# One-hot gate matrix, top-k selection and rank inversion in 16 bits, with the gate in three 16-bit parts

## The chip, the cores and the metric

The kernel runs on one core of a Trainium2 chip. The metric is device time in microseconds (us); less is better. The core has five engines with a queue each: PE (TensorE, matmuls into the PSUM banks; its weight loads are a row of their own, PEld), DVE (VectorE, elementwise and reductions), ACT (ScalarE, activations, copies and scalings), POOL (GpSimd, here almost only a queue that issues DMAs) and SP (a queue that issues DMAs). An engine works through its queue in order; semaphores make it wait for other engines and for DMAs.

## The reference, cut to what matters

One encoder block over 256 tokens of width 2048: modulation, mixer (convolution and attention), and then a PEER layer, in which every token takes 16 of 16384 experts for each of 8 heads:

```python
scores = einsum('bshpd,hpnd->bshpn', q, sub_keys)          # two halves, 128 keys each
top_v, top_i = top_k(scores, 16)
cand = top_v[..., 0, :, None] + top_v[..., 1, None, :]      # 16 x 16 per head
best_v, best_i = top_k(cand, 16)
i1 = take_along_axis(top_i[..., 0, :], best_i // 16)
i2 = take_along_axis(top_i[..., 1, :], best_i % 16)
expert, gate = i1 * 128 + i2, softmax(best_v)
a   = einsum('td,tnd->tn', h, peer_u[expert])
out = einsum('tn,tnd->td', gelu(a) * gate, peer_v[expert])
```

## The kernel before, in words

The kernel does not gather rows of `peer_u`. In its **block loop** it multiplies all 256 tokens with all 128 blocks of 128 experts: for a block, 1 MB of `peer_u` comes in on SP's queue (`ru`, 4 buffers `wraw`), ACT rounds it to `hu` (L198), DVE makes the remainder `lu` (L199), and PE runs 48 matmuls of 128x256 (`mm3`: L213 and L214 with `hu`, then L217 with `lu`) into `pu`. ACT writes GELU of it to `A` (L1185). `hu` and `lu` have two buffers each.

Beside this stream runs the **gate part** (`side_steps`), a generator that the block loop advances by a budget: every block pays SIDE = 3.3, and each `yield` says what its step costs, so this table of costs sets how many steps stand between two blocks. A Tile scheduler then orders each engine's queue. Its steps, for each half of 128 tokens (`tt`): top-k of the 256 sums (`cand`), selection of the indices with a one-hot `eq` (L927 compares, L931 multiplies, L933 sums), softmax, a transpose through PE (`selT`, L944), and then the **gate matrix**: for each token a 128x128 matrix with the gate at (i2, i1), as a product of two one-hot matrices. In steps of four tokens DVE compares a counter `iota` with `i2T` and with `i1T` (`oh_make`, L869, two instructions of 512 elements), ACT scales the second one by the gate, token by token (L872), PE multiplies (`oh_use`, L882, one f32 matmul per token), ACT copies the result to `stage` (L884), and after each 16 tokens DVE takes the largest value over them (L890 or L893), which tells the sort which experts are in use. HOLD = 2 says how many steps lie between the making and the use of a one-hot pair. The gate part has the first UPART = 48 blocks; what is left of it then is issued at once.

In the later blocks a second generator, `sort_steps`, orders the experts by which token groups use them. It ends with the **inversion** of the ranks: 32 steps of four one-hot rows, two comparisons (L1090), two products (L1092, L1093) and four matmuls of 128x256 in 16 bits (L1082). At the same time `ask` and `weigh` bring the gate matrix back, multiply it into `A` and put the result to HBM (`actd`); both issue on POOL's queue. At block EARLY_AT = 118 seven gathers of 1 MB of `peer_v` (`fetch_raw`, `rv` and `early`) go onto POOL's queue, and behind them the load `bt` of the last gate's bias, for which four additions on DVE (L977) wait.

After the block loop comes the **product stage** (`po`, L1228 and L1236): for each sorted block 1 MB of `peer_v` and its weights (`mc`) are gathered through POOL's queue and multiplied. Then the sum, the last norm and the output.

Of the kernel before, what the change touches and what calls it, by code (L numbers as in the profile page):

```python
# [21 lines left out]
T = 256  # L22
# [7 lines left out]
UPART = 48  # L30
ABUFS = 7
E2BUFS = 4
HOLD = 2
# [21 lines left out]
EARLY_AT = NBLK - 10  # L55
# [75 lines left out]
def hybrid_block_kernel(  # L131
# [34 lines left out]
    def ps_tile(name):  # L166
# [5 lines left out]
    iota = cst.tile([128, 128], F32, name="iota")  # L172
    nc.gpsimd.iota(iota, pattern=[[1, 128]], base=0, channel_multiplier=0,
                   allow_small_or_imprecise_dtypes=True)
# [68 lines left out]
    with tc.tile_pool(name="pre", bufs=1) as pre:  # L243
# [5 lines left out]

        vec = pre.tile([128, NVEC], F32, name="vec")  # L250
# [566 lines left out]
    sifs = [tks[:, 1024 + i * 256:1280 + i * 256].rearrange("p (h k) -> p h k", k=16) for i in range(2)]  # L817

    def m1(name, dt=F32):
        return sp.tile([128, 256], dt, tag="m1", name=name, bufs=5)  # L820
# [36 lines left out]
    i1T, i2T, gT = [m1(n) for n in ("i1T", "i2T", "gT")]  # L857
# [4 lines left out]
    def oh_make(tt, q):  # L862
        t = tt * 128 + q * 4
        it = iota.unsqueeze(1).to_broadcast([128, 4, 128])
        ohs = []
        for i, src in enumerate((i2T, i1T)):
            oh = e2(f"oh{tt}_{q}") if i else work[:, 2048 + 512 * ((32 * tt + q) % 3):][:, :512]
            oh = oh.rearrange("p (t i) -> p t i", t=4)
            V.tensor_tensor(oh, it, src[:, t:t + 4].unsqueeze(2).to_broadcast([128, 4, 128]), ALU.is_equal)  # L869
            ohs.append(oh)  # L870
        for j in range(4):
            S.activation(ohs[1][:, j], ohs[1][:, j], AF.Copy, scale=gT[:, t + j:t + j + 1])  # L872
        return ohs

    def oh_use(tt, q, ohs):
        tb, qq = divmod(q, TB // 4)
        if qq == 0:
            stages[tt, tb] = g8(f"stage{tt}_{tb}", (128, 128, TB))
        stage = stages[tt, tb]
        p = ps_tile(f"gps{tt}_{q}")  # L880
        for j in range(4):
            keep(PE.matmul(p[:, j * 128:(j + 1) * 128], lhsT=ohs[0][:, j], rhs=ohs[1][:, j],  # L882
                          start=True, stop=True))
        S.activation(stage[:, :, qq * 4:(qq + 1) * 4].rearrange("p i t -> p t i"),  # L884
                     p.rearrange("p (t i) -> p t i", t=4), AF.Copy)
        if qq == TB // 4 - 1:
            S.dma_start(gd[tt * (128 // TB) + tb], stage)
            gm = picked[:, 4 * tt + tb * TB // 32]
            if tb * TB % 32 == 0:
                V.tensor_reduce(gm, stage, AX.X, ALU.max)  # L890
            else:
                mx = e2(f"mx{tt}_{tb}")[:, :128]
                V.tensor_reduce(mx, stage, AX.X, ALU.max)  # L893
                V.tensor_tensor(gm, gm, mx, ALU.max)

    def side_steps():
# [5 lines left out]
        for tt in range(2):  # L902
# [16 lines left out]
            for which in range(2):  # L919
                if which == 0:  # L920
                    V.tensor_single_scalar(bs, bi, 4, ALU.logical_shift_right)
                else:
                    V.tensor_single_scalar(bs, bi, 15, ALU.bitwise_and)
                bf = tk[:, 1536:1664].rearrange("p (h k) -> p h k", k=16)
                V.tensor_copy(bf, bs)
                eq = g8(f"eq{tt}_{which}", (128, 8, 16, 16))
                V.tensor_tensor(eq, bf.unsqueeze(3).to_broadcast([128, 8, 16, 16]),  # L927
                                iota[:, :16].unsqueeze(1).unsqueeze(1).to_broadcast([128, 8, 16, 16]),
                                ALU.is_equal)
# [16 lines left out]
            V.tensor_copy(i1T[:, ts_], pt[:, 0:128])  # L946
            V.tensor_copy(i2T[:, ts_], pt[:, 128:256])
            V.tensor_copy(gT[:, ts_], pt[:, 256:384])
            yield 1.0
            for q in range(32):  # L950
# [4 lines left out]
                yield 1.2  # L955
# [26 lines left out]
    def sort_steps():  # L982
        nk = len(CLASSES) + 1
        cls = work[:, 2048:2048 + 64 * nk].bitcast(BF).rearrange("p (k i) -> p k i", k=nk)
        flat = sp.tile([128, 512], BF, tag="m1", name="tri", bufs=5)
# [86 lines left out]
        plo = work[:, 1024:1280].rearrange("p (c i) -> p c i", c=2)  # L1072
        V.tensor_copy(plo[:, 0], ri)
        V.tensor_copy(plo[:, 1], rj)
        yield 5.0
        pi = ps_tile("inv")
        it = iota.unsqueeze(1).to_broadcast([128, 4, 128])
        late = None

        def invert(ch, oh, vals):  # L1080
            for i in range(4):
                keep(PE.matmul(pi[:, :256], lhsT=oh[:, 0, i], rhs=vals[:, i].rearrange("p a b -> p (a b)"),  # L1082
                              start=(ch == 0 and i == 0), stop=(ch == 31 and i == 3)))

        for ch in range(32):
            isl = slice(ch * 4, (ch + 1) * 4)
            oh = sp.tile([128, 2, 4, 128], BF, tag="e2", name=f"sl{ch}", bufs=E2BUFS)
            vals = sp.tile([128, 4, 2, 128], BF, tag="e2", name=f"sv{ch}", bufs=E2BUFS)
            for i in range(2):
                V.tensor_tensor(oh[:, i], it, plo[:, i, isl].unsqueeze(2).to_broadcast([128, 4, 128]),  # L1090
                                ALU.is_equal)
            V.tensor_scalar(vals[:, :, 0], oh[:, 1], pidx, None, ALU.mult)  # L1092
            V.tensor_tensor(vals[:, :, 1], oh[:, 1], iota[:, isl].unsqueeze(2).to_broadcast([128, 4, 128]),  # L1093
                            ALU.mult)
# [3 lines left out]
            yield 2.4  # L1098
# [80 lines left out]
    for i1 in range(NBLK):  # L1179
# [260 lines left out]
```

## Time and profile before

| | |
|---|---|
| median of 3 runs | 1761.83 us (1760.68 to 1767.35) |
| profiled execution, whole | 1762.56 us |
| its span, first to last instruction | 1760.8 us |
| PE busy | 1683.4 us (96%) |
| DVE busy | 1200.5 us (68%) |
| ACT busy | 761.6 us (43%) |
| block loop | 565.5 to 1387.6 us |
| gate matrix of the first and the second 128 tokens | 641.1 to 743.6 and 800.5 to 910.5 us |

A matmul's recorded duration holds its way through the array, so the rate of PE is read from the starts of matmuls that follow one another, and what a stage costs from its length. In a timeline row the first number is the start and the second the length of a run of equal instructions, with the idle time before it and what ended it in brackets. In a row of groups come the count, then the busy time in us and the mean ns of one, then the engine's idle time before.

### The profile page before, as it was taken

The page shows a single profiled execution, that of the slowest core. Times are in us where ns is not written, and L with a number is a line of the kernel's source. Part 1 is how long each engine was busy: PE and PEld are TensorE (multiplying, and loading weights), DVE is VectorE, ACT ScalarE, POOL GpSimd, SP SyncE. Part 2 cuts the span into 40 slices and gives each one's busy share as a digit, 9 for nine tenths or more (in the row PEclk, how much of TensorE's full clock was granted, in tenths as well). Part 3 has the DMA queues.
Part 4 walks back from the last instruction along what each step waited for, and adds up shares of the span by engine and source line. Part 5 has one row for each costly group of instructions (what it writes and reads, how often), then busy time and mean ns, then how long its engine had stood idle before and what let it go on. Part 6 is the DMA issues. An engine that isn't in the chain of part 4 may idle for free. (4 is left out here: it accounts for less than half of the span.)

```text
span 1760.8 us, 29506 instructions
## 1 busy us (share of the span) xinstructions
PE 1683.4 (96%) x12507; PEld 1461.9 (83%) x12507; DVE 1200.5 (68%) x1605; ACT 761.6 (43%) x1016; POOL 288.1 (16%) x257
## 2 busy tenths in 40 slices
PE   4998999899999999999999999999999999999996
PEld 2778999899899999899999999999999754444542
DVE  6769899778667988897885788898744332222324
ACT  3233467334544468847974343333433232222322
POOL 0000000000000000000000000000030476756771
PEclk8988999899999999999999999999999999999998
DMA  9998888679555455546569887888988599998895
GB/s 396 425 375 298 324 331 304 244 277 348 207 217 180 158 182 212 195 175 219 198 233 347 284 307 255 296 298 286 322 311 317 219 393 393 354 361 336 307 395 217
DMA packets 77928, 505.93 MB, mean 287 GB/s; under 512 B 9472, under 2 KB 10112, under 8 KB 22496
## 3 DMA queue, kind: packets, MB, share of 16 engines
q1 hardware_dynamic: 44784, 319.82, 48.2%
q0 software_dynamic: 29712, 162.94, 25.3%
q10 hardware_dynamic: 3296, 21.24, 3.0%
q8 instruction: 100, 1.64, 0.4%
q14 instruction: 36, 0.29, 0.0%
HBM read 466.21 MB, written 37.75 MB: 286 GB/s over the span
## 5 line engine op out<-in xcount | busy, mean ns | idle before, releaser
L213 PE MATMUL pu<-h2hi,hu 128*128 128x256 f32 x2048 | 497.8, 284 | 0.0
L198 ACT ACTIVATE hu<-ru 128x2048 fp32r<-128x2048 f32 x128 | 245.4, 1917 | 365.7 <-PE pu L214 316.7
L213 PEld LDWEIGHTS pu<-h2hi,hu 128*128 128x128 f32 x2048 | 386.0, 188 | 0.6 <-issue 0.2
L199 DVE TENSOR_TENSOR lu<-ru,hu 128x2048 fp32r<-128x2048 f32 x128 | 293.1, 2291 | 135.6 <-ACT hu L198 133.4
L217 PE MATMUL pu<-h2hi,lu 128*128 128x256 f32 x2048 | 263.2, 281 | 0.5 <-DVE lu L199 0.5
L217 PEld LDWEIGHTS pu<-h2hi,lu 128*128 128x128 f32 x2048 | 251.3, 188 | 0.7 <-DVE lu L199 0.7
L214 PE MATMUL pu<-h2loT3a,hu 128*128 128x256 f32 x1024 | 249.4, 282 | 0.0
L214 PE MATMUL pu<-h2loT3b,hu 128*128 128x256 f32 x1024 | 247.9, 281 | 0.0
L1228 PE MATMUL po<-rv,mc 128*64 128x512 f32 (+2 forms) x1064 | 225.5, 600 | 5.2 <-PEq L1310 2.6
L1228 PEld LDWEIGHTS po<-rv,mc 128*64 128x64 f32 (+2 forms) x1064 | 72.6, 131 | 147.0 <-issue 140.5
L214 PEld LDWEIGHTS pu<-h2loT3a,hu 128*128 128x128 f32 x1024 | 193.2, 189 | 0.2 <-issue 0.2
L214 PEld LDWEIGHTS pu<-h2loT3b,hu 128*128 128x128 f32 x1024 | 192.9, 188 | 0.0
L1125 POOL DMA_DIRECT2D gg<-gd x16 | 18.7, 1169 | 914.9 <-DVE work L1002 914.6
L1170 POOL DMA_INDIRECT rv<-in_peer_v_dram,perm_idx x107 | 129.1, 1207 | 77.1 <-PE po L1228 33.2
L204 DVE TENSOR_TENSOR lv<-rv,hv 128x2048 fp32r<-128x2048 f32 x24 | 55.1, 2294 | 122.5 <-ACT hv L203 89.9
L1177 POOL DMA_INDIRECT mc<-actd,perm_idx x109 | 121.1, 1111 | 37.1 <-issue 30.8
L241 DVE SCALAR_TENSOR_TENSOR acc<-ada,cact,acc 128x2048 f32<-128x2048 f32 x45 | 105.7, 2348 | 3.4 <-DMA ada<-in_w_ada_dram 3.4
L203 ACT ACTIVATE hv<-rv 128x2048 fp32r<-128x2048 f32 x24 | 45.9, 1913 | 130.6 <-DMA rv<-in_peer_v_dram,perm_idx 118.4
L198 ACT ACTIVATE hwin<-rwin 128x2048 fp32r<-128x2048 f32 x33 | 63.0, 1910 | 66.1 <-DMA rwin<-in_w_in_dram 40.0
L213 PE MATMUL pwin<-hhi,hwin 128*128 128x256 f32 x336 | 88.4, 301 | 0.0
L872 ACT ACTIVATE oh<-oh,gT 128x128 f32<-128x128 f32 x256 | 80.8, 390 | 14.8 <-DVE oh L869 14.1
L204 DVE TENSOR_TENSOR third<-rv,third 128x2048 fp32r<-128x2048 f32 x12 | 27.6, 2299 | 87.3 <-ACT third L203 53.7
(522 smaller groups left out, 3036.3 us busy)
## 6 DMA issues: line engine op xcount, KB each, us to landing
ru<-in_peer_u_dram SPq DMA_DIRECT2D x128, 1024.0 KB, 5.4
ada<-in_w_ada_dram SPq DMA_DIRECT2D x96, 1024.0 KB, 7.4
rwin<-in_w_in_dram SPq DMA_DIRECT2D x33, 1024.0 KB, 6.1
rwout<-in_w_out_dram SPq DMA_DIRECT2D x16, 1024.0 KB, 5.3
rwq<-in_w_q_dram SPq DMA_DIRECT2D x16, 1024.0 KB, 4.8
gd<-stage ACTq DMA_DIRECT2D x16, 1024.0 KB, 5.0
gg<-gd POOLq DMA_DIRECT2D x16, 1024.0 KB
actd<-A POOLq DMA_DIRECT2D x15, 1024.0 KB
```

Of the source, the lines that this page charges most:

```text
L198: S.activation(hi, raw, AF.Copy)
L199: V.tensor_tensor(lo, raw, hi.bitcast(F32), ALU.subtract)
L203: S.activation(hi, src, AF.Copy)
L204: V.tensor_tensor(lo, src, hi.bitcast(F32), ALU.subtract)
L213: PE.matmul(dst, lhsT=whi[:, sl], rhs=rhi[:, c], start=(c == sets[0][0]), stop=False)
L214: PE.matmul(dst, lhsT=whi[:, sl], rhs=rlo[:, c], start=False, stop=False)
L217: PE.matmul(dst, lhsT=wlo[:, sl], rhs=rhi[:, c], start=False, stop=(c == sets[-1][-1]))
L241: V.scalar_tensor_tensor(acc, raw, cact[:, k:k + 1], acc, ALU.mult, ALU.add)
L872: S.activation(ohs[1][:, j], ohs[1][:, j], AF.Copy, scale=gT[:, t + j:t + j + 1])
L1170: keep(nc.gpsimd.indirect_dma_start(raw, None, v_rows, index(main[n])))
L1177: keep(nc.gpsimd.indirect_dma_start(ms[-1][:, n % 8], None, actd[:, :], index(main[n])))
L1228: keep(PE.matmul(po[tt * 4 + d4][row:row + size], lhsT=m[:, at * size:(at + 1) * size], rhs=raw[:, d4 * 512:(d4 + 1) * 512], start=start, ...
```

## The change

The counter `iota`, the indices and the one-hot matrices become 16-bit, and every index is written twice side by side (`twice`), so that the comparison with a row reads pairs of neighbouring 16-bit values on all three sides (`hot`). The steps of the gate matrix hold eight tokens in place of four (OHB). ACT's scaling goes; instead the gate is split into three 16-bit parts that add up to it (`gT` with three columns per token), one DVE instruction makes the three scaled one-hot matrices of eight tokens (3072 elements), and PE adds three 16-bit matmuls per token where one f32 matmul stood. The one-hot matrix for i2 moves from `work` to the `e2` buffers, the three products take two buffers in `work`, HOLD is 1, and the step's cost in the table is 2.6. The selection's `eq` and its index factor are 16-bit. The inversion has 16 steps of eight rows; its matmuls are 256 of 128x128 in place of 128 of 128x256. UPART is 50, and the seven early gathers are spread over the blocks 114 to 126, one at each even one; the rest of the sort is issued at 114.

```diff
-UPART = 48
+UPART = 50
-HOLD = 2
+HOLD = 1
+OHB = 8
-EARLY_AT = NBLK - 10
+EARLY_AT = (114, 116, 118, 120, 122, 124, 126)
...
+    i1T, i2T = [sp.tile([128, T, 2], BF, tag="m1", name=n, bufs=2) for n in ("i1T", "i2T")]
+    gT = sp.tile([128, T, 3, 2], BF, tag="gT", name="gT")
+
+    def hot(dst, idx):
+        n = idx.shape[1]
+        V.tensor_tensor(dst.rearrange("p n (a b) -> p n a b", b=2),
+                        pairs_of(iota).unsqueeze(1).to_broadcast([128, n, 64, 2]),
+                        idx.unsqueeze(2).to_broadcast([128, n, 64, 2]), ALU.is_equal)
+
+    def twice(x):
+        return x.unsqueeze(2).to_broadcast([128, x.shape[1], 2])
...
     def oh_make(tt, q):
-        t = tt * 128 + q * 4
-        it = iota.unsqueeze(1).to_broadcast([128, 4, 128])
-        for i, src in enumerate((i2T, i1T)):
-            oh = e2(f"oh{tt}_{q}") if i else work[:, 2048 + 512 * ((32 * tt + q) % 3):][:, :512]
-            V.tensor_tensor(oh, it, src[:, t:t + 4].unsqueeze(2).to_broadcast([128, 4, 128]), ALU.is_equal)
-        for j in range(4):
-            S.activation(ohs[1][:, j], ohs[1][:, j], AF.Copy, scale=gT[:, t + j:t + j + 1])
+        t = tt * 128 + q * OHB
+        oh2, oh1 = [e2(f"oh{i}_{tt}_{q}").bitcast(BF).rearrange("p (t i) -> p t i", t=OHB) for i in (2, 1)]
+        og = work[:, 1024 + 1536 * (q % 2):2560 + 1536 * (q % 2)].bitcast(BF).rearrange("p (t c i) -> p t c i", t=OHB, c=3)
+        hot(oh2, i2T[:, t:t + OHB])
+        hot(oh1, i1T[:, t:t + OHB])
+        V.tensor_tensor(og.rearrange("p t c (a b) -> p t c a b", b=2),
+                        oh1.rearrange("p t (a b) -> p t a b", b=2).unsqueeze(2).to_broadcast([128, OHB, 3, 64, 2]),
+                        gT[:, t:t + OHB].unsqueeze(3).to_broadcast([128, OHB, 3, 64, 2]), ALU.mult)
+        return oh2, og
...
         for j in range(4):
-            keep(PE.matmul(p[:, j * 128:(j + 1) * 128], lhsT=ohs[0][:, j], rhs=ohs[1][:, j],
-                          start=True, stop=True))
+            for c in range(3):
+                keep(PE.matmul(p[:, j * 128:(j + 1) * 128], lhsT=ohs[0][:, t0 + j], rhs=ohs[1][:, t0 + j, c],
+                              start=(c == 0), stop=(c == 2)))
...
+            left = tk[:, 1792:1920]
+            V.tensor_copy(gT[:, ts_, 0], twice(pt[:, 256:384]))
+            V.tensor_tensor(left, pt[:, 256:384], gT[:, ts_, 0, 0], ALU.subtract)
+            V.tensor_copy(gT[:, ts_, 1], twice(left))
+            V.tensor_tensor(left, left, gT[:, ts_, 1, 0], ALU.subtract)
+            V.tensor_copy(gT[:, ts_, 2], twice(left))
-            for q in range(32):
+            for q in range(128 // OHB):
...
-                yield 1.2
+                yield 2.6
...
-        for ch in range(32):
+        for ch in range(16):
...
-        if i1 == EARLY_AT:
+        if i1 == EARLY_AT[0]:
             for _ in side:
                 pass
-            for n in range(EARLY):
-                fetch_raw(n)
+        if i1 in EARLY_AT:
+            fetch_raw(EARLY_AT.index(i1))
```

**DVE, gate matrix of the first 128 tokens, before** (`lu` is the remainder of a block's weights, `work<-iota,i2T` and `oh_n` the two one-hot matrices of a step of four tokens):

```order
L199 TENSOR_TENSOR lu_6843<-ru_6840,hu_6842 128x2048
L869 TENSOR_TENSOR work<-iota,i2T 128x512
L869 TENSOR_TENSOR oh_8_6727<-iota,i1T 128x512
L869 TENSOR_TENSOR work<-iota,i2T 128x512
L869 TENSOR_TENSOR oh_9_6797<-iota,i1T 128x512
L199 TENSOR_TENSOR lu_6927<-ru_6924,hu_6926 128x2048
L893 TENSOR_REDUCE mx_1_6810<-stage_1_6706 128x128
L869 TENSOR_TENSOR work<-iota,i2T 128x512
```

The same place now (`oh_0_k` twice is the pair of step k, i2 first; `work<-oh,gT` is the product with the three gate parts):

```order
L198 TENSOR_TENSOR lu_6966<-ru_6963,hu_6965 128x2048
L910 TENSOR_REDUCE mx_1_6835<-stage_1_6715 128x128
L866 TENSOR_TENSOR oh_0_5_6894<-iota,i2T 128x1024
L911 TENSOR_TENSOR work<-work,mx_1_6835 128x128
L866 TENSOR_TENSOR oh_0_5_6895<-iota,i1T 128x1024
L866 TENSOR_TENSOR oh_0_6_6928<-iota,i2T 128x1024
L882 TENSOR_TENSOR work<-oh_0_5_6895,gT 128x3072
L198 TENSOR_TENSOR lu_7056<-ru_7053,hu_7055 128x2048
```

The comparison for step 6 now stands ahead of step 5's product, and the product is DVE's where ACT had it.

**PE, the end of step 4 and the beginning of step 5 there, now** (`gps` is a PSUM bank of four tokens, with three matmuls and three weight loads per token):

```order
L899 LDWEIGHTS oh_0_4_6801
L899 MATMUL gps_9_6914<-work,oh_0_4_6801 128x128
L899 LDWEIGHTS oh_0_5_6894
L899 MATMUL gps_10_6933<-work,oh_0_5_6894 128x128
L899 LDWEIGHTS oh_0_5_6894
L899 MATMUL gps_10_6933<-work,oh_0_5_6894 128x128
```

Two steps stand next to each other on PE, with no block between them; this is so at six places (steps 0 and 1, 4 and 5, 9 and 10 of the first half; 1 and 2, 5 and 6, 10 and 11 of the second), and everywhere else one block of 48 matmuls stands between two steps. Before, PE's queue had up to three banks of four tokens in a row, and single matmuls of a bank between single ones of a block.

**POOL, around the early gathers, now** (`actd` puts weighed `A` tiles, `gg` asks for gate matrix, `bt` is the bias):

```order
L1195 DMA rv_14023<-in_peer_v_dram,perm_idx 128x2048
L1195 DMA rv_14137<-in_peer_v_dram,perm_idx 128x2048
L1150 DMA gg_14251<-gd 128x16x128
L1195 DMA rv_14253<-in_peer_v_dram,perm_idx 128x2048
L994 DMA bt<-in_b_gtf_dram 128x2048
L1195 DMA rv_14382<-in_peer_v_dram,perm_idx 128x2048
L1161 DMA actd<-A_13851 128x8x256
L1150 DMA gg_14498<-gd 128x16x128
L1195 DMA rv_14500<-in_peer_v_dram,perm_idx 128x2048
```

Before, all seven gathers stood in one run ahead of `bt`; now three stand ahead of it.

More of the change, by code (lines that the diff above doesn't have):

```diff
@@ L816, in hybrid_block_kernel @@
            for i in range(2)]
-    sifs = [tks[:, 1024 + i * 256:1280 + i * 256].rearrange("p (h k) -> p h k", k=16) for i in range(2)]
-    def m1(name, dt=F32):
-        return sp.tile([128, 256], dt, tag="m1", name=name, bufs=5)
+    sifs = [tks[:, 1024 + i * 128:1152 + i * 128].bitcast(BF).rearrange("p (h k) -> p h k", k=16)
+            for i in range(2)]
     def e2(name):
@@ L923, in side_steps @@
                     V.tensor_single_scalar(bs, bi, 15, ALU.bitwise_and)
[L924 to L929, printed above, removed]
+                bf = tk[:, 1536:1664].bitcast(BF).rearrange("p (n b) -> p n b", b=2)
+                V.tensor_copy(bf, twice(bs.rearrange("p h k -> p (h k)")))
+                eq = g8(f"eq{tt}_{which}", (128, 8, 16, 16), BF)
+                V.tensor_tensor(eq.rearrange("p h k (a b) -> p (h k) a b", b=2),
+                                bf.unsqueeze(2).to_broadcast([128, 128, 8, 2]),
+                                pairs_of(iota[:, :16]).unsqueeze(1).to_broadcast([128, 128, 8, 2]), ALU.is_equal)
                 yield 2.5
@@ L984, in sort_steps @@
         cls = work[:, 2048:2048 + 64 * nk].bitcast(BF).rearrange("p (k i) -> p k i", k=nk)
-        flat = sp.tile([128, 512], BF, tag="m1", name="tri", bufs=5)
+        flat = sp.tile([128, 512], BF, tag="m1", name="tri", bufs=2)
         tri, ones_bf, tot = flat[:, 0:128], flat[:, 128:256], flat[:, 256:256 + nk]
@@ L1078, in sort_steps @@
+        V.tensor_copy(iota2, twice(iota))
         late = None
         def invert(ch, oh, vals):
-            for i in range(4):
-                keep(PE.matmul(pi[:, :256], lhsT=oh[:, 0, i], rhs=vals[:, i].rearrange("p a b -> p (a b)"),
-                              start=(ch == 0 and i == 0), stop=(ch == 31 and i == 3)))
-        for ch in range(32):
[L1086 to L1094, printed above, removed]
+            for i in range(8):
+                for a in range(2):
+                    keep(PE.matmul(pi[:, a * 128:(a + 1) * 128], lhsT=oh[:, i], rhs=vals[a][:, i],
+                                  start=(ch + i + a == 0), stop=(ch == 15 and i == 7), skip_group_check=True))
@@ new lines, in sort_steps @@
+        for ch in range(16):
+            isl = slice(ch * 8, (ch + 1) * 8)
+            flats = ([work[:, 2048 + 512 * n:2560 + 512 * n] for n in range(4)] if ch % 2 else
+                     [e2(f"s{n}{ch}") for n in range(4)])
+            oh, oj, *vals = [x.bitcast(BF).rearrange("p (i j) -> p i j", i=8) for x in flats]
+            hot(oh, plo[:, 0, isl])
+            hot(oj, plo[:, 1, isl])
+            V.tensor_scalar(vals[0], oj, pidx, None, ALU.mult)
+            V.tensor_tensor(vals[1].rearrange("p i (a b) -> p i a b", b=2),
+                            oj.rearrange("p i (a b) -> p i a b", b=2),
+                            iota2[:, isl].unsqueeze(2).to_broadcast([128, 8, 64, 2]), ALU.mult)
```

37 lines of the change are left out of this document (19 added, 18 removed).

## The prediction

> **What bounds the kernel now.** I read the cores first, then the busy time by stage, then the starts of matmuls and the groups of the gate stretches.
>
> ```profile
> core 0: 1760.8 us, clock 0.979
> 565.50:641.10 75.60, 75.60 (x642) 75.60 (x641) 70.08 (x158) 34.46 (x33) 0.00 (x0) 1.00 0.49 180
> 641.10:743.60 102.50, 97.72 (x820) 96.54 (x819) 84.90 (x92) 88.67 (x180) 0.00 (x0) 1.00 0.57 206
> 743.60:800.50 56.90, 56.90 (x483) 56.90 (x482) 52.40 (x89) 27.17 (x28) 0.00 (x0) 1.00 0.51 178
> 800.50:910.50 110.00, 106.02 (x902) 105.25 (x901) 91.13 (x95) 96.18 (x189) 0.00 (x0) 1.00 0.59 208
> 910.50:1387.60 477.10, 476.53 (x4034) 470.84 (x4033) 344.59 (x342) 177.79 (x159) 46.21 (x42) 1.00 0.82 295
> 1387.60:1760.80 373.20, 355.29 (x1622) 169.48 (x1620) 113.29 (x111) 89.88 (x94) 241.34 (x210) 0.98 0.88 340
> ```
>
> After the stretch and its length the columns are PE, weight loads, DVE, ACT and POOL busy, the granted clock and the DMAs. In the stretches of top-k (565.5, 743.6) and in the long one of the sort PE has no idle time, whatever DVE does; only the two of the gate matrix have some (4.8 and 4.0 us). So the block loop is PE's. A time saved on DVE or ACT counts only in the two gate stretches; elsewhere only what PE itself does less counts.
>
> A block's own time is the distance of two equal rows on ACT in a quiet place, 1285.07 - 1279.39 = 5.68 us:
>
> ```profile
> 1279.39 1.92 ACT L198 ACTIVATE hu<-ru 128x2048 fp32r<-128x2048 f32 x1 [3.40 <-PE pu L214]
> 1285.07 1.92 ACT L198 ACTIVATE hu<-ru 128x2048 fp32r<-128x2048 f32 x1 [3.40 <-PE pu L214]
> ```
>
> What the matmuls around the change cost on PE stands in the starts of its rows:
>
> ```profile
> 654.37 2.84 PE L882 MATMUL gps<-oh,work 128*128 128x128 f32 x24
> 656.97 0.36 PE L213 MATMUL pu<-h2hi,hu 128*128 128x256 f32 x1
> ...
> 996.75 0.39 PE L1059 MATMUL rank<-tri 128*128 128x128 bf16 x4
> 996.95 0.37 PE L213 MATMUL pu<-h2hi,hu 128*128 128x256 f32 x1
> ...
> 1062.04 0.61 PE L1082 MATMUL inv<-sv,sl 128*128 128x256 bf16 x4
> 1062.41 0.36 PE L213 MATMUL pu<-h2hi,hu 128*128 128x256 f32 x1
> ```
>
> An f32 matmul of the gate has two records, so 24 records are 12 tokens in 2.60 us: 0.217 us a token. Four 16-bit matmuls of 128 columns took 0.20 us; I take 0.0555 each, since the four of 256 columns took 0.37 and the first block matmul behind such a run costs 0.08 more (0.20 to its successor in place of 0.12): (0.37 + 0.08)/4 = 0.11 for twice the columns.
>
> The groups of the first gate stretch tell how near the other engines are to PE:
>
> ```profile
> L872 ACT ACTIVATE oh<-oh,gT 128x128 f32<-128x128 f32 x125 | 39.1, 390 | 4.1 <-DVE oh L869 3.9 <-ACT oh L872 0.2
> L882 PE MATMUL gps<-oh,work 128*128 128x128 f32 x239 | 31.9, 281 | 4.8 <-ACT oh L872 4.7
> L199 DVE TENSOR_TENSOR lu<-ru,hu 128x2048 fp32r<-128x2048 f32 x12 | 27.5, 2289 | 7.0 <-ACT hu L198 7.0
> L869 DVE TENSOR_TENSOR work<-iota,i2T 128x512 f32<-128x512 f32 x32 | 22.0, 688 | 9.8 <-PE gps L882 9.8
> L890 DVE TENSOR_REDUCE work<-stage 128x128 f32<-128x2048 f32 x4 | 9.1, 2285 | 0.7 <-ACT stage L884 0.7
> ```
>
> PE's idle time ends with ACT's scaling, the end of a chain DVE, ACT, PE. The stretch has 12 blocks (12 `lu`) and 120 tokens (240 records); the second one, counted likewise, 13 blocks and 136 tokens. Beyond the blocks the two cost 102.5 - 12 x 5.68 + 110.0 - 13 x 5.68 = 70.5 us. The matmuls are 256 x 0.217 = 55.5 of it; 15.0 are waits and changes between the two kinds of matmul.
>
> **The change, part by part.** *Gate matmuls:* 768 x 0.0555 = 42.6 us in place of 55.5: -12.9 on PE, which sets the end.
>
> *DVE and ACT in the gate stretches.* ACT loses 256 scalings of 390 ns; with 88.67 of 102.50 it was close to the end, and is it no longer. DVE gets the product. No row before has a product or comparison with all sides in 16 bits; the nearest are:
>
> ```profile
> L1093 DVE TENSOR_TENSOR sv<-sl,iota 128x512 bf16<-128x512 bf16 x32 | 21.9, 686 | 0.0
> L1092 DVE TENSOR_SCALAR sv<-sl,pidx 128x512 bf16<-128x512 bf16 x32 | 11.3, 353 | 0.9
> ```
>
> Two f32 inputs took 688 ns for 512 elements and 2289 for 2048: 1.043 ns an element and 0.153 us fixed. At that rate, which L1093 has as well (there the counter is still f32), 1024 elements take 1.22 us and 3072 take 3.36, and a step of eight tokens 2 x 1.22 + 3.36 = 5.80 us. L1092, all 16-bit but one input, has (353 - 153)/512 = 0.39 ns: 0.55 and 1.35, a step of 2.46. I take half the f32 rate, 0.52 ns, nearer to L1092 since every side is 16-bit with neighbours in pairs: 0.69 and 1.75, a step of **3.13 us** (before: 4 x 0.688 = 2.75 on DVE and 8 x 0.39 on ACT).
>
> The Trainium skill, VectorE: DVE Perf Modes, section "The perf-mode tier table", gives a tensor_tensor with 16-bit sides in SBUF two elements per cycle, 1224 ns for 2048 elements; no run here shows it yet. By that page a step would be an estimated 3.13 us too.
>
> DVE's sum over both stretches, which with the longer gate part hold 27 blocks in the new order: 27 x 2.29 + 32 x 3.13 + 16 reductions x 2.28 + 6 for small ones = 204.5 us. PE's: 27 x 5.68 + 42.6 = 196.0. Before, with two more blocks: 212.5 + 11.4 = 223.9. So DVE is now the fuller engine, and PE can't have the whole of its own saving. What is late next is seen where two steps stand next to each other on PE. DVE's comparison for step 6 waits until PE has finished step 4 and so freed an `e2` buffer (four buffers, two a step, one for a maximum); only then come that comparison and step 5's product, 0.69 + 1.75 = 2.45 us, in which PE stands. At the first of the six places both products are made two blocks ahead. Five remain: 5 x 2.45 = 12.2 us. Elsewhere a block lies between two steps, 5.68 us of cover; without it each would cost PE the same 2.45. Add 25 changes from 16-bit to block matmuls at 0.08 = 2.0. The gate costs 42.6 + 12.2 + 2.0 = 56.8 in place of 70.5: **-13.7**. The 15.0 us of waits thus stay much what they were, with another cause.
>
> *Inversion:* before 32 x (0.37 + 0.08) = 14.4 us on PE; now 256 x 0.0555 + 16 x 0.08 = 15.5: **+1.1**. The DVE time that it saves is not on the path, nor that of the 16-bit top-k, as PE's full rows there show.
>
> *Early gathers and `bt`:*
>
> ```profile
> 1346.75 2.49 DVE L977 TENSOR_TENSOR gtf<-gtfp,bt 128x512 f32<-128x512 f32 x4 [12.00 <-DMA bt<-in_b_gtf_dram]
> 1347.20 0.38 ACT L1185 ACTIVATE A<-pu 128x256 f32<-128x256 f32 x1
> 1353.69 0.39 ACT L1185 ACTIVATE A<-pu 128x256 f32<-128x256 f32 x1 [0.25 <-PE pu L217]
> ```
>
> DVE stood 12 us for `bt`, which lay behind seven gathers; `lu` was late, and a block took 6.49 us, 0.81 too long. With three gathers ahead of it `bt` is in time: **-0.8**; at worst 0. The seventh gather now comes just ahead of the product stage. Its block is the seventh in the order, behind the 16 f32 matmuls of the two blocks that need no gather; I cost it at nothing, and at 3 us (1 MB at the 340 GB/s of that stage) if that cover fails.
>
> *Waits added elsewhere:* what they would hold up are loads and puts of 1 MB:
>
> ```profile
> ru<-in_peer_u_dram SPq DMA_DIRECT2D x128, 1024.0 KB, 5.4
> gd<-stage ACTq DMA_DIRECT2D x16, 1024.0 KB, 5.0
> ```
>
> The sort's limits go by SP into a part of `work` that a gate product now uses, so SP waits for the last gate matmul, with `ru` loads queued behind it. The first of these is for the fourth block after that matmul. PE has three blocks, 17 us, in between, and `ru` lands 5.4 us after its issue: nothing; without those blocks some 5 us. The later `ask` leaves three blocks between the first `weigh` and the reuse of its `A` tile, 17 us for a put of 1 MB (5.0 us for `stage`): nothing, some 5 us if not. The small copies behind `selT` run under the two blocks that follow it.
>
> Sum: -13.7 + 1.1 - 0.8 = -13.4 against the profiled span of 1760.8, so 1747.4. That execution took 1762.56, the median is 1761.83, 1.0 above the span: **1748.4 us**.
>
> **The rivals.** *DVE takes one 16-bit element at a time* (slower). For it: L1093 kept the f32 rate with a 16-bit output; each index is a repeated pair, not a run. Against: there one side was f32, and the pairs make every side contiguous by two. Then DVE needs 27 x 2.29 + 32 x 5.80 + 36.5 + 6 = 290 us where 223.9 were: +66, with the inversion 1827 to 1829. It decides from a step of (223.9 - 104.3)/32 = 3.74 us; above that the gate part is slower than before.
>
> *The shorter hand-over costs at every step* (no change). HOLD 1 and four `e2` buffers let DVE be only one step ahead. If besides the five places each of the other 20 groups of steps waits for one comparison of 0.69 us, 13.8 us go and the time is 1762. For it: DVE already waited 9.8 us for PE's release of `work`. Against: a block of 5.68 us covers it.
>
> *The waits between steps vanish*, and DVE's sum of 204.5 sets the stretches: -19.4, 1742 to 1743. Against it stands the order on DVE.
>
> *16-bit weight loads don't overlap* (slower). All 768 matmuls load weights anew, and the record of one such load is 98 ns:
>
> ```profile
> L1082 PEld LDWEIGHTS <-sl 128*128 128x128 bf16 x128 | 10.0, 98 | 2.2
> ...
> 961.61 0.75 PE L1014 MATMUL clstot<-tri,work 128*128 128x1 bf16 x24
> 962.23 0.36 PE L213 MATMUL pu<-h2hi,hu 128*128 128x256 f32 x1
> ```
>
> At 0.098 each PE needs 153.4 + 75.3 + 2 = 230.7 us for 223.9, and the inversion 26.4 for 14.4: about 1780. Against it: 24 matmuls of one column with 24 loads took 0.62 us, so a load behind a load costs 0.026.
> The Trainium skill, TensorE: Matmul & The Clock Gate, section "Back-to-back issue gap", has some 81 ns for a matmul of 128 columns in a stream of loads and matmuls. This trace's four in 0.20 us differ; by that page the time would be an estimated 1762.
>
> **How the numbers follow.** Forecast 0.62 (1743 to 1756 by the bounds of a step and of the covers), one element at a time 0.10, waits at every step 0.13, no waits 0.11, loads 0.04. A measurement of this kernel tells a change from none at about 0.5%: below 1753 or above 1771. Faster: most of the forecast and the case without waits, 0.68. No change: the rest of the forecast and the waits at every step, 0.18. Slower: 0.14. The range 1738 to 1762 holds the forecast, the case without waits and nearly all of the waits at every step; the two slow cases lie outside.
>
> **What would show it.** DVE's groups in the gate stretches: about 0.69 us for 1024 elements and 1.75 for 3072; 1.22 and 3.36 would be the first rival. PE: starts of the gate's matmuls 0.055 us apart; idle time ended by DVE's product, some 2.5 us each at five places and nothing at the others. Two gate stretches of about 211 us for 27 blocks. The inversion at 0.9 us a step. No wait of DVE for `bt`. I am wrong if a stage other than these moves by more than 3 us, above all the product stage.

## The result and the profile after

The changed kernel takes 1744.65 us (median of five runs, 1742.80 to 1751.59) where the kernel before took 1761.83 us beside it: a ratio of 0.9914, 95% interval 0.9894 to 0.9933. Beside three of the experiments it was run again: 1740.82 us against 1758.37, ratio 0.9890 (0.9868 to 0.9911). The forecast was 1748.4 us, range 1738 to 1762. The total was met to 4 us, but by two errors of opposite sign: the waits between the steps of the gate matrix, for which 12.2 us stood in the sum, hardly exist, and a wait that costs 6 us stands at a place that the sum had at nothing.

First comes the busy time by stage of the changed kernel (the stretch, its length, then PE, weight loads, DVE, ACT and POOL busy, the granted clock, DMA share and GB/s); the second and fourth stretch hold the gate matrix, the fifth the sort, the sixth the products:

```profile
565.87:637.60 71.73, 71.73 (x609) 71.73 (x608) 65.35 (x158) 32.79 (x32) 0.00 (x0) 1.00 0.53 189
637.60:745.90 108.30, 107.95 (x1097) 107.30 (x1096) 104.00 (x96) 63.97 (x60) 0.00 (x0) 1.00 0.63 215
745.90:801.70 55.80, 55.80 (x486) 55.76 (x485) 46.96 (x84) 26.55 (x24) 0.00 (x0) 1.00 0.54 189
801.70:902.60 100.90, 100.90 (x1050) 100.31 (x1049) 96.66 (x78) 63.61 (x61) 0.00 (x0) 1.00 0.63 227
902.60:1369.30 466.70, 462.12 (x4019) 458.62 (x4023) 306.29 (x274) 171.80 (x153) 46.85 (x42) 1.00 0.83 295
1369.30:1741.00 371.70, 353.48 (x1622) 166.99 (x1620) 113.20 (x111) 89.88 (x94) 246.41 (x210) 0.99 0.88 342
```

PE has no idle time left in the gate stretches (0.35 us in both together); DVE is at 96% of them, ACT down to some 60%. The idle time of PE now stands in the fifth stretch, 4.6 us of it. What PE waited for in the whole block loop (us in total, times, the longest), of the kernel before and of the changed one:

```profile
PE gps L882 <- ACT oh L872: 8.7, 9, 1.8
PE pu L217 <- DVE lu L199: 0.5, 1, 0.5
```

```profile
PE pu L216 <- DVE lu L198: 4.2, 1, 4.2
PE gps L899 <- DVE work L882: 0.3, 1, 0.3
```

The nine waits for ACT's scaling are gone, and one single wait of 4.2 us for `lu` is new. DVE's groups in the gate stretches (count, busy time, mean ns of one, idle before) have the durations of the forecast, 0.69 and 1.75 us, and the selection's comparison and product of 2048 elements went from 2.29 to 1.22 us (the last row is the comparison):

```profile
L882 DVE TENSOR_TENSOR work<-oh,gT 128x3072 bf16<-128x3072 bf16 x32 | 56.0, 1753 | 0.2
L866 DVE TENSOR_TENSOR oh<-iota,i1T 128x1024 bf16<-128x1024 bf16 x32 | 22.0, 686 | 0.2
L866 DVE TENSOR_TENSOR oh<-iota,i2T 128x1024 bf16<-128x1024 bf16 x32 | 21.9, 684 | 0.0
...
L944 DVE TENSOR_TENSOR eq<-tk,iota 128x2048 bf16<-128x2048 bf16 x2 | 2.4, 1222 | 0.0
```

The place where a wait was most expected, two steps next to each other on PE (steps 4 and 5 of the first 128 tokens), on DVE and then on PE:

```profile
674.64 0.69 DVE L866 TENSOR_TENSOR oh<-iota,i1T 128x1024 bf16<-128x1024 bf16 x1
675.25 0.69 DVE L866 TENSOR_TENSOR oh<-iota,i2T 128x1024 bf16<-128x1024 bf16 x1
675.85 1.75 DVE L882 TENSOR_TENSOR work<-oh,gT 128x3072 bf16<-128x3072 bf16 x1
677.52 2.29 DVE L198 TENSOR_TENSOR lu<-ru,hu 128x2048 fp32r<-128x2048 f32 x1
```

```profile
675.80 1.51 PE L899 MATMUL gps<-work,oh 128*128 128x128 bf16 x24
677.66 1.51 PE L899 MATMUL gps<-work,oh 128*128 128x128 bf16 x24 [0.35 <-DVE work L882]
```

The row at 675.25 is the comparison for step 6. It starts before PE has begun step 4 (675.80), so it did not wait for it; the product for step 5 follows at once, and PE stands 0.35 us. At the five other places with 48 matmuls in a row the two steps took 2.66 to 2.70 us, which is 48 x 0.055 or a little more. Nor does DVE stand for PE anywhere here: its waits between 641 and 900 us (in total, times, the longest) all end with ACT.

```profile
DVE lu L198 <- ACT hu L197: 11.8, 4, 3.5
DVE lu L198 <- ACT A L1210: 3.7, 1, 3.7
DVE mx L910 <- ACT stage L901: 0.8, 3, 0.4
```

The new wait is in the sort's stretch. In order of time: the last gate matmuls, the put of their `stage` to the gate matrix in HBM (`gd`), the gather of the first `gg` from it on POOL, the first weighing on DVE with the `lu` rows around it, and the matmuls on PE that need the second of these `lu`:

```profile
896.18 1.51 PE L899 MATMUL gps<-work,oh 128*128 128x128 bf16 x24
```

```profile
899.11 0.33 ACTq L904 DMA_DIRECT2D gd<-stage  x1
```

```profile
910.00 1.34 POOL L1150 DMA_DIRECT2D gg<-gd  x1 [908.83 <-DMA gd<-stage]
```

```profile
910.29 2.29 DVE L198 TENSOR_TENSOR lu<-ru,hu 128x2048 fp32r<-128x2048 f32 x1
922.58 2.29 DVE L1156 TENSOR_TENSOR A<-A,gg 128x2048 f32<-128x2048 f32 x1 [10.01 <-DMA gg<-gd]
926.15 2.28 DVE L198 TENSOR_TENSOR lu<-ru,hu 128x2048 fp32r<-128x2048 f32 x1
```

```profile
928.49 3.24 PE L216 MATMUL pu<-h2hi,lu 128*128 128x256 f32 x16 [4.23 <-DVE lu L198]
```

From the last gate matmuls (they end at 896.18 + 1.32 = 897.5) to the weighing are 25.1 us. DVE stands 10 us of them at the weighing, with `lu` queued behind it, and PE runs out of `lu`: the block that starts at 920.31 and its successor take, from first matmul to first matmul, 11.21 + 6.18 us instead of 2 x 5.68, 6.0 us too long. In the kernel before three `lu` stood between the last maximum and the first weighing, and the gather was there when DVE came to it; now two stand there.

**The ledger of the block loop.** It went from 822.07 to 803.43 us (from the first matmul of the first block to the first of the product stage), by 18.6 us:

| term | forecast | came | from |
|---|---|---|---|
| gate matrix | -13.7 | -25.4 | 26 runs of gate matmuls, 43.0 us from start to next block, + 26 changes x 0.08 = 45.1 instead of 70.5 |
| first weighing | 0 | +6.0 | the two long blocks |
| inversion | +1.1 | +1.0 | 16 x (0.88 + 0.08) = 15.4 instead of 14.4 |
| `bt` | -0.8 | -0.8 | the block that took 6.49 now takes 5.68 |
| not assigned | | +0.6 | |

Read from the lengths of the blocks instead (what each has over 5.68 us), the gate matrix is 24.8 us less and the inversion 0.7 more, and 0.3 us is left over; so the terms are good to about 0.7 us. The rest of the span moved by 1.1 us (start of the loop 565.5 to 565.87, product stage 373.2 to 371.7).

### The profile page after: what moved, and what is told of

It is laid out like the page before. It is cut to its first block, busy times and chain, and to the rows that moved or that the text cites. A ratio compares the mean times of both kernels' runs of the same rounds, so it can differ in the third digit from the quotient of the medians.

```text
span 1741.0 us, 29854 instructions
## 1 busy us (share of the span) xinstructions
PE 1664.9 (96%) x12886; PEld 1446.6 (83%) x12891; DVE 1176.6 (68%) x1519; ACT 696.5 (40%) x760; POOL 293.8 (17%) x257
## 3 DMA queue, kind: packets, MB, share of 16 engines
q8 instruction: 102, 1.67, 0.4%
## 5 line engine op out<-in xcount | busy, mean ns | idle before, releaser
L1202 POOL DMA_INDIRECT mc<-actd,perm_idx x109 | 130.3, 1195 | 36.2 <-issue 31.8
L213 PE MATMUL pwin<-hlo,hwin 128*128 128x256 f32 x336 | 85.6, 293 | 0.0
```

What stands on the lines that cost most here:

```text
L213: PE.matmul(dst, lhsT=whi[:, sl], rhs=rlo[:, c], start=False, stop=False)
L1202: keep(nc.gpsimd.indirect_dma_start(ms[-1][:, n % 8], None, actd[:, :], index(main[n])))
```

## The experiments

The stages outside the loop are the same code in all of these kernels, but for the place of the early gathers; yet the loop began between 562.95 and 572.54 us and the product stage took 367.6 to 371.7 us, with no relation to the edit. So the loop's length, read from one profile, is the sharper measure; the times carry the verdict where they can. The medians of the kernel before, beside the five sets of runs, were 1761.83, 1758.63, 1758.37, 1756.93 and 1757.28 us.

| kernel | time, us | ratio to the kernel before (95%) | block loop, us |
|---|---|---|---|
| changed kernel | 1744.65 | 0.9914 (0.9894 to 0.9933) | 803.4 |
| the same again | 1740.82 | 0.9890 (0.9868 to 0.9911) | 805.6 |
| first weighing a block later | 1733.05 | 0.9857 (0.9839 to 0.9875) | 797.4 |
| gate part to block 48 | 1740.40 | 0.9890 (0.9873 to 0.9906) | 804.1 |
| two of three matmuls a token | 1736.60 | 0.9860 (0.9835 to 0.9884) | 799.8 |
| two of three parts on DVE | 1742.80 | 0.9896 (0.9869 to 0.9922) | 803.6 |
| two parts on both, weighing later | 1722.67 | 0.9785 (0.9767 to 0.9803) | 783.2 |
| 256 columns, weighing later | 1730.77 | 0.9838 (0.9822 to 0.9854) | 796.2 |
| hold 0 | 1770.38 | 1.0059 (1.0037 to 1.0080) | 835.0 |
| kernel before without scaling | 1745.94 | 0.9932 (0.9912 to 0.9951) | 810.1 |
| single index | 1808.72 | 1.0298 (1.0274 to 1.0323) | 874.2 |
| early gathers at 118 | 1737.51 | 0.9882 (0.9862 to 0.9901) | 804.2 |
| gate to 48, 256 columns, weighing later | 1732.93 | 0.9856 (0.9840 to 0.9872) | 796.4 |

**The first weighing, one block later**

```diff
-            weighs.setdefault(at, []).append(k)
+            weighs.setdefault(at + (k == 0), []).append(k)
```

> Changed kernel, its first weigh one block later (block 54; its gather is asked for at block 50 as before). Theory W: the 6.0 us that PE stands at the fifth block after the last gate matmul are the first weigh, which waits on DVE for its gather ahead of that block's lu. One more block of cover is 5.68 us, so at most 0.3 us of the wait is left: 1744.65 - 5.7 = 1739.0 us, and no block near it longer than 6.5 us. Rival R: the lu there is late for another reason (its ru load, or the sort's work on DVE): the long block stays and the time is 1744 to 1745. Rival T: the later put of the weighed tile now holds up the tile that takes its place: the wait moves by two or three blocks, and the time is 1742 to 1745.

The loop is 797.38 us, 6.05 less than the changed kernel's; the blocks around the place take 5.68 to 5.77 us. DVE still waits for the gather, but now behind one more `lu`, and PE does not notice (the last row is its only wait in the loop):

```profile
919.54 2.29 DVE L1156 TENSOR_TENSOR A<-A,gg 128x2048 f32<-128x2048 f32 x1 [4.99 <-DMA gg<-gd]
921.75 4.49 DVE L198 TENSOR_TENSOR lu<-ru,hu 128x2048 fp32r<-128x2048 f32 x2
```

```profile
PE gps L899 <- DVE work L882: 0.4, 1, 0.4
```

Theory W holds, and neither rival does: the wait went away and came back nowhere else. The ratio, 0.9857, is 0.6% below the changed kernel's in its first set and 0.3% in its second, where the intervals overlap by a hair; the next runs with this edit bear it out.

**The gate part to block 48, as before**

```diff
-UPART = 50
+UPART = 48
```

> Changed kernel with the gate part of the stage ending at block 48 in place of 50; what is left of the gate is then done at once at block 48. Theory W: the first weigh stands ahead of the lu of the fourth block after the last gate matmul instead of the fifth, with the same chain of put and gather behind that matmul (25 us), so its wait grows by one block: 6.0 + 5.7 = 11.7 us, the time 1750.3 us. Rival R (the stall is not of the weigh): the stall stays at 6 us and the time is 1744 to 1746. A third: work done at once at block 48 makes PE stand for DVE's products, some 3.1 us for each of one or two steps: up to 1756.

The loop took 804.09 us, 0.7 more than the changed kernel's, not 5.7. One `lu` less does stand ahead of the weighing, but the two long blocks were only 6.5 us too long (11.46 and 6.37 us), because the gather took less time: issued at 906.71 it was there at 914.76, 8.0 us, where the changed kernel's took 12.6 (910.00 to 922.58).

```profile
906.71 1.34 POOL L1150 DMA_DIRECT2D gg<-gd  x1 [905.54 <-DMA ru<-in_peer_u_dram]
```

```profile
914.76 2.29 DVE L1156 TENSOR_TENSOR A<-A,gg 128x2048 f32<-128x2048 f32 x1 [8.19 <-DMA gg<-gd]
```

So the wait stays at the weighing, and my price for a block less was wrong, since it took the chain as fixed. By the time alone rival R (a stall of 6 us as before) does as well; it is the run above that rules it out. A gate part of two blocks more is worth nothing by itself.

**PE's share or DVE's share of the third part left out**

Two runs, each with one engine relieved. On PE:

```diff
-            for c in range(3):
+            for c in range(2):
                 keep(PE.matmul(p[:, j * 128:(j + 1) * 128], lhsT=ohs[0][:, t0 + j], rhs=ohs[1][:, t0 + j, c],
-                              start=(c == 0), stop=(c == 2)))
+                              start=(c == 0), stop=(c == 1)))
```

> Changed kernel, leaving out the matmul with the third 16-bit part of the gate (512 gate matmuls in place of 768); DVE still makes all three parts. Theory P: PE sets the two gate stretches and finds its products ready, so the 256 matmuls of 0.0555 us come off the time: 1744.65 - 14.2 = 1730.4 us. Rival D: DVE's sum (204.5 us of work in the two stretches) sets them, PE's waits grow by what its matmuls lose, and the time stays at 1743 to 1745. Between: each us less than 14.2 is a us in which PE now stands for DVE.

On DVE (not shown: `gT`, `og` and the other factor lose their third part likewise, and the two instructions that make that part go):

```diff
...
-                        gT[:, t:t + OHB].unsqueeze(3).to_broadcast([128, OHB, 3, 64, 2]), ALU.mult)
+                        gT[:, t:t + OHB].unsqueeze(3).to_broadcast([128, OHB, 2, 64, 2]), ALU.mult)
...
-                keep(PE.matmul(p[:, j * 128:(j + 1) * 128], lhsT=ohs[0][:, t0 + j], rhs=ohs[1][:, t0 + j, c],
+                keep(PE.matmul(p[:, j * 128:(j + 1) * 128], lhsT=ohs[0][:, t0 + j], rhs=ohs[1][:, t0 + j, c % 2],
```

> Changed kernel, in which DVE makes only two of the three 16-bit parts of the gate (product of 2048 in place of 3072 elements) and the third matmul of a token takes the first part again, so that PE does all 768 matmuls. DVE has 32 x (1.75 - 1.22) = 17 us less. Theory P (PE sets the gate stretches): no change, 1744 to 1745 us, at most the 0.5 us by which one pair of steps waited. Rival D (DVE's sum sets them): up to 17 us less, down to 1728.

With PE relieved of 14.2 us the loop is 3.7 us shorter; with DVE relieved of 17 us (its product took 1217 ns) it stays, 803.62 us: its gate blocks are 0.6 us shorter and its stall at the weighing 0.8 us longer. PE sets the gate stretches, theory P, but DVE is only some 4 us behind: what PE's matmuls lose beyond that turns into waits for the product,

```profile
PE gps L899 <- DVE work L882: 7.5, 5, 3.4
PE pu L216 <- DVE lu L198: 4.1, 1, 4.1
PE gps L899 <- ACT A L1210: 0.9, 2, 0.5
```

where the middle row is the first weighing again. The two other rows are 8.4 of the 10.5 us that did not come; the rest goes with slower work behind the longest of these waits, where the granted clock was 0.79 (683 to 691 us). So relieving PE ended in between the two theories, and nearer to D.

**The third part left out on both engines**, with the first weighing a block later (the changes of the three runs above together):

> Changed kernel with the first weigh at block 54 and without the third 16-bit part of the gate on either engine: the gate is held to two parts, 512 matmuls and a product of 2048 elements. Leaving the matmuls out alone took 3.7 us off the block loop, leaving DVE's part out alone none. Theory B (both engines are close to the bound in the gate stretches, DVE some 4 us behind PE): with both out the whole 14.2 us come, on top of the 6 of the weigh: block loop 803.4 - 6.0 - 14.2 = 783 us, 0.977 of the kernel before. Rival D (something else on DVE, lu and the reductions, holds PE): less than 8 us beyond the weigh, 789 us or more, 0.981 to 0.985.

The loop took 783.21 us; 783 had been worked out. PE works in 782.71 of it, and DVE's relief, worth nothing alone, brings the 10 us that PE's alone did not:

```profile
569.21:1352.42 783.21, 782.71 (x7000) 777.83 (x6999) 602.02 (x683) 358.42 (x328) 46.32 (x42) 1.00 0.74 266
```

This kernel computes less: the gate is held to two 16-bit parts. It is no version to set beside the others without asking whether that is enough.

**Hold 0: a step's matmuls right behind its product**

```diff
-HOLD = 1
+HOLD = 0
```

> Changed kernel with a step's matmuls standing right behind its own product in the order (hold 0 in place of 1), so that DVE's lead over PE is one step of 3.13 us less; buffers and work are the same. Theory H (the lead of DVE is what keeps PE from standing, and a place with two steps together leans on it): PE stands up to 3.13 us at each of the five places of that kind, 10 to 16 us in all: 1755 to 1760 us. Rival N (a block of 5.68 us between steps and the buffers give the lead anyway): under 2 us, 1743 to 1746.

The loop is 835.0 us, 31.5 more, twice what theory H had; nothing is left of rival N. PE's waits in the loop:

```profile
PE gps L899 <- DVE work L882: 26.3, 8, 7.4
PE pu L216 <- DVE lu L198: 1.2, 1, 1.2
```

These waits are not 3.13 us at the five double places: only one of the eight, the longest, is between two steps that stand together, and seven are ahead of a step that stands alone, where DVE was still at other work of its queue or at the step itself. The stall at the weighing does not occur in this run, so the gate part lost more than the loop shows: by the lengths of its blocks 36 us, the waits and the slower work behind them (granted clock 0.81 from 655 to 664 us). The lead of one step is thus what the whole gate part lives on, and HOLD 1 was enough of it.

**The kernel before without ACT's scaling**

```diff
-        for j in range(4):
-            S.activation(ohs[1][:, j], ohs[1][:, j], AF.Copy, scale=gT[:, t + j:t + j + 1])
```

> The kernel before, leaving out ACT's 256 scalings (the gate factor is missing from its output); f32 matmuls, DVE's comparisons, hold 2 and all the rest stay. Theory S: the 15.0 us of waits and changes in its gate part come of the third hand-over DVE, ACT, PE, so without it the 8.8 us of PE's idle time go and some of the rest: 9 to 13 us less, 1745 to 1750 us, against 25.5 us that the whole change took off the gate part, 12.9 of them by the shorter matmuls. Rival V: DVE's comparisons come too late themselves (each waits for PE to free a third of the work buffer); PE then waits for DVE in place of ACT, and under 3 us go: 1755 to 1759.

The loop fell from 822.07 to 810.13 us, by 11.9, and PE does not wait once for the 512 records of the gate:

```profile
L880 PE MATMUL gps<-oh,work 128*128 128x128 f32 x512 | 61.1, 275 | 0.0
```

Theory S holds: with the same f32 matmuls, the same comparisons and HOLD 2 the scaling alone was the cause of the waits. So the 25.4 us of the gate part are, by difference, two halves: about 12.9 by the shorter matmuls, and about 12 by taking ACT's scaling out. The run takes away the hand-over to ACT and ACT's work together (ACT was busy in 88.67 of the 102.50 us of the first gate stretch before), so it doesn't say which of the two made PE wait.

**One stored element in place of a pair**

```diff
-                        idx.unsqueeze(2).to_broadcast([128, n, 64, 2]), ALU.is_equal)
+                        idx[:, :, 0:1].unsqueeze(2).to_broadcast([128, n, 64, 2]), ALU.is_equal)
...
-                        gT[:, t:t + OHB].unsqueeze(3).to_broadcast([128, OHB, 3, 64, 2]), ALU.mult)
+                        gT[:, t:t + OHB, :, 0:1].unsqueeze(3).to_broadcast([128, OHB, 3, 64, 2]), ALU.mult)
```

> Changed kernel, with the comparisons and the gate product reading each index and each gate part once and repeating that one element over 128 columns (step 0 innermost) in place of a stored pair repeated 64 times; outputs and counter stay 16-bit. Theory E: it is the pair that lets DVE take two elements at a time; without it 1024 elements take 1.22 us and 3072 take 3.36, a step of eight tokens 5.80 us, DVE becomes the bound of the gate stretches, and the time is 1810 to 1830 us. Rival Q: 16-bit data is enough, the durations stay 0.69 and 1.75 us, and the time at 1741 us.

```profile
L882 DVE TENSOR_TENSOR work<-oh,gT 128x3072 bf16<-128x3072 bf16 x32 | 107.0, 3347 | 0.0
L866 DVE TENSOR_TENSOR oh<-iota,i1T 128x1024 bf16<-128x1024 bf16 x32 | 38.8, 1212 | 0.0
```

Theory E holds: the types and the elements are the same, and the instructions take 1212 and 3347 ns, the rate of f32. PE waits 53.7 us for the product, and the kernel is 3% slower than the one before. The time is 1808.7, a little under the range given. The Trainium skill, Vector Engine (DVE) Microarchitecture Reference, section "Performance modes — why throughput varies by op and dtype", asks for a step of one and more than one element in the innermost dimension of every 16-bit side for two results a cycle; a pair is the least that meets it, and by the two runs a pair is enough.

**The early gathers together at block 118**

```diff
-EARLY_AT = (114, 116, 118, 120, 122, 124, 126)
+EARLY_AT = (118,)
...
-            fetch_raw(EARLY_AT.index(i1))
+            for n in range(EARLY):
+                fetch_raw(n)
```

> Changed kernel with its seven early gathers asked for together at block 118, as in the kernel before, in place of one at every second block from 114. Theory G: the load of bt stands behind them again, DVE waits some 12 us for it, and one block takes 6.5 us in place of 5.68: 0.8 us more in the block loop; the product stage keeps its length within 1 us. Rival: the 1.9 us by which the product stage was shorter in the changed kernel come of the earlier gathers, and it gets longer by that too, 2.7 us in all. Both lie near the limit of what the times can tell; the trace tells them apart.

The wait is back, in the trace alone:

```profile
L999 DVE TENSOR_TENSOR gtf<-gtfp,bt 128x512 f32<-128x512 f32 x4 | 2.5, 683 | 11.7 <-DMA bt<-in_b_gtf_dram 11.7
```

In the changed kernel this row has no idle time:

```profile
L999 DVE TENSOR_TENSOR gtf<-gtfp,bt 128x512 f32<-128x512 f32 x4 | 2.5, 682 | 0.0
```

A block behind the wait took 6.19 us instead of 5.68; the loop is 804.2, 0.8 us more than the changed kernel's, though that is less than its two profiles differ by. The product stage took 368.4 us (1738.8 - 1370.4), less than the changed kernel's 371.7 (1.5 us, and not 1.9, below the kernel before), so nothing speaks for the rival; but kernels with the same gathers differ by 4 us there, and one profile can't rule out an effect of 2. The times can't tell this edit from none.

**The inversion in matmuls of 256 columns**, with the first weighing a block later:

```diff
-                for a in range(2):
-                    keep(PE.matmul(pi[:, a * 128:(a + 1) * 128], lhsT=oh[:, i], rhs=vals[a][:, i],
...
+                keep(PE.matmul(pi[:, :256], lhsT=oh[:, i], rhs=vals[i // 4][:, i % 4].rearrange("p a b -> p (a b)"),
...
```

> Changed kernel with the first weigh at block 54 and the inversion's matmuls put back to 256 columns (8 a step in place of 16 of 128, the values of a token's two digits side by side). The kernel before took (0.37 + 0.08)/4 us for one such matmul with the change to the block behind it, or 0.0925 in the run itself. Theory: a step is 8 x 0.0925 + 0.08 = 0.82 us in place of 0.96, so 16 steps give 2.3 us: block loop 797.4 - 2.3 = 795.1 us. Rival: in long runs 256 columns cost twice 128 (0.11 us), 0.88 + 0.08 a step, and nothing is gained: 797 us.

A step of the inversion, of the changed kernel and of this one, with the block matmul behind it:

```profile
1057.08 1.07 PE L1106 MATMUL inv<-s,s 128*128 128x128 bf16 x16
1057.96 0.36 PE L212 MATMUL pu<-h2hi,hu 128*128 128x256 f32 x1
```

```profile
1051.62 1.05 PE L1105 MATMUL inv<-s,s 128*128 128x256 bf16 x8
1052.42 0.36 PE L212 MATMUL pu<-h2hi,hu 128*128 128x256 f32 x1
```

From start to start these are 0.88 and 0.80 us, so 0.055 for 128 columns and 0.100 for 256. The loop is 1.2 us shorter than with the weighing alone (796.2 after 797.4); 2.3 had been expected. The 0.0925 of the kernel before came from a run of four, too short for a rate.

**The changed kernel again**

> The changed kernel itself once more, beside the three others on their chip, since the kernel before took 1761.83 and 1758.63 us in two sets of runs. Every theory expects a ratio of about 0.9914 and, in its trace, a block loop of 803 to 804 us with a stall of about 6 us at the first weigh.

The ratio is 0.9890 and the loop 805.6 us. The stall is 8.2 us here (blocks of 12.71 and 6.85), with the gather issued at 910.25 and the weighing at 924.08, 13.8 us: the size of the stall is the gather's, and varies from run to run.

**The gate part to 48, the later weighing and 256 columns** (the changes of three runs above together)

> Changed kernel with the gate part ending at block 48 as in the kernel before, the first weigh one block later than that rule puts it (block 52, the fifth block after the last gate matmul again having lu ahead of weigh) and the inversion in matmuls of 256 columns. Theory L (the two blocks more buy nothing by themselves; all that counts is how many blocks stand between the last gate matmul and the first weigh): block loop 804.1 - 6.5 - 1.2 = 796.4 us, as in the run with the gate part to block 50 (796.2), ratio 0.984. Rival M: with the gate part two blocks shorter the chain of put and gather still ends behind the weigh, as it took from 20 to 28 us in the runs so far: up to 4 us of the wait are left, 800 us.

The loop took 796.41 us, as theory L has it to the tenth. The gather was quick in this one too (907.06 to 914.70). Block 50 or 48 makes no difference to the loop; the place of the first weighing does. The fastest kernels that compute all of it are this one and the one with the gate part to 50: 1732.93 and 1730.77 us, ratios 0.9856 and 0.9838. The times don't tell them from the later weighing alone (1733.05 us, 0.9857). The second ran beside the changed kernel and was 10 us below it (1730.77 and 1740.82).

## Why the prediction was right and where it was wrong

*What bounds the kernel:* right. The block loop is PE's, before and after.

*Gate matmuls, -12.9:* right. 24 of them take 1.32 us, 0.055 each; the rival in which weight loads don't overlap is out. The Trainium skill's 81 ns (TensorE: Matmul & The Clock Gate, "Back-to-back issue gap") don't fit these runs of 16 to 48 matmuls with a fresh load each; the 55.6 ns that its Part 1 gives for back-to-back matmuls do.

*DVE's step, 3.13 us:* the durations were right to 0.01 us. As a sum for the stretches they were too much: an instruction starts 0.08 us before the one ahead of it has its recorded end (675.25, 675.85, 677.52 in the rows above: 0.60 and 1.67 from start to start), so a step occupies DVE 2.87 us. With 0.08 off each of some 140 instructions the sum of 204.5 us is about 193, below PE's 196 + 2. "DVE is now the fuller engine" is the sentence that fell, if narrowly: relieved of 17 us, DVE gave PE nothing.

*Five places x 2.45 = 12.2 us:* **the step that failed.** It said that the comparison for step 6 waits until PE has finished step 4, because the four `e2` buffers go round two a step. But of a step's two one-hot matrices only one is read by PE, the other by DVE's own product alone, and the buffers taken by the maxima shift the round; at the place shown the comparison took a buffer that DVE itself had freed, and waits for no other engine. Other comparisons do take a buffer that PE read, but PE had always finished that step: DVE has no wait for PE in the rows above. So DVE stays a whole step ahead, and 0.5 us came of the 12.2. What a lead one step shorter costs, the run with hold 0 shows: 26.3 us of waits. The rival in which the waits vanish had that much right, and its time of 1742 to 1743; its other half, that DVE's sum then sets the stretches, is not so.

*Where the waits before came from:* the prediction read them rightly as the end of a chain DVE, ACT, PE, but let them "stay much what they were, with another cause". Without the scaling they are gone, and the loop is 11.9 us shorter.

*Waits added elsewhere, nothing:* wrong at one of two places. For the later `ask` I looked at the put behind the first weighing and the reuse of its tile (that held), and not at the gather ahead of it, which can only start after the last gate matmul's put. 25.1 us of chain stood against two `lu` of cover: +6.0, 8.2 in the second profile. By the prediction's own sign (a stage other than those named moves by more than 3 us) this part of it was wrong. The load of the sort's limits behind the last gate matmul did no harm.

*Inversion +1.1 and `bt` -0.8:* right, +1.0 and -0.8. *Seventh gather, nothing:* right; the product stage took no longer.

*One 16-bit element at a time,* as a rival at 1827 to 1829: with a single stored index it is 1808.7, 52 us above the kernel before beside it and not 66; some 11 of the 14 us between are the same 0.08 us for each of about 140 instructions. That its condition was not met here is shown by the durations.

Against the forecast the gate came out 11.7 us lower and the weighing 6.0 us higher. The two errors partly cancel, and both are small beside the range: that it held was in part luck, and not because the account was right.

## What to carry to other kernels

When work goes from a chain of three engines to a chain of two, ask what the last engine's waits for the middle one cost, and not only what the work costs: here taking the middle one out gave about as much as the faster matmuls. Whether a buffer round makes one engine wait for another is settled by who reads each buffer and which step it was, buffer by buffer; a count of buffers is not enough. And when the last producer of a round trip through memory moves later, follow the trip to its first consumer and count the instructions that its engine has ahead of it: moving that consumer by one place was worth a third of the whole change.

## What the runs showed of the chip

A wait can cost PE more than its length. The wait of 4.23 us at the weighing made two blocks 6.0 us longer; in the stretches around it the granted clock (seventh of the columns) falls behind the wait:

```profile
924.20:928.40 4.20, 0.06 (x1) 0.00 (x0) 4.20 (x13) 0.00 (x0) 2.67 (x2) 1.00 0.26 93
928.40:932.60 4.20, 4.11 (x22) 4.12 (x23) 3.29 (x5) 2.30 (x2) 0.00 (x0) 0.59 0.98 277
932.60:938.00 5.40, 5.40 (x47) 5.40 (x47) 3.77 (x2) 0.00 (x0) 0.00 (x0) 1.00 1.01 366
```

In the kernel with a single index a wait of 2.75 us did the same, 0.69 over the next 4.6 us. In the block loops of these runs no wait of up to 1.75 us was followed by a lower clock, and every one of 3.41 us and more was. Between the two it went either way: in the run with hold 0 two waits of 2.12 us had 0.62 and 1.00 behind them:

```profile
730.56:735.06 4.50, 4.50 (x37) 4.50 (x38) 4.50 (x4) 2.15 (x2) 0.00 (x0) 0.62 0.22 71
851.48:855.98 4.50, 4.50 (x51) 4.50 (x52) 4.50 (x4) 2.02 (x2) 0.00 (x0) 1.00 0.29 66
```

The mean clock of the loop was 0.97 with a single index and 1.00 in the changed kernel. The Trainium skill, TensorE: Matmul & The Clock Gate, Part 1, has the clock halve after an idle window of some 3.4 us and come back after as long a busy one. The waits of 3.41 us and more agree; those of 2.11 to 2.89 us that a lower clock followed were shorter than that window, and there the measurement decides.

The first gather of a `gg`, 1 MB, took 8.0 and 7.6 us from issue to the weighing in the two runs of the changed kernel with the gate part to block 48, and 12.0 to 14.3 in the ten with it to block 50. In the kernel before without scaling, to block 48 too, it took 9.2. So the longer gather goes with the later end of the gate part in every run; what it shares the DMA engines with in each was not tested, and the cause stays open. It is why the stall at the first weighing has no fixed size.
